# Delta rule: decay matrices kept in device memory, and four products tied into one run

## The chip, the cores and the metric

The kernel runs on one core of a Trainium2 chip. The metric is device time in microseconds, the median of three runs. A core has TensorE (PE in the profile, its weight loads PEld), VectorE (DVE), ScalarE (ACT), GpSimd (POOL) and SyncE (SP); each works through its own list of instructions in order. Here SyncE issues nearly all DMA transfers, and ScalarE a few.

## The reference

Two layers of a decoder trunk on 512 tokens of width 1024, all in float32. Each layer normalises x, makes one wide projection, and runs three branches side by side: a Mamba-2 scan, latent attention, and a gated delta rule. Their outputs are projected, gated, merged and projected again; a feed-forward part follows. The change lies in the delta rule, which in the reference has chunks of 64 tokens:

```
g = jnp.cumsum(chunks(g), axis=-1)
decay = jnp.exp(jnp.where(incl, g[..., :, None] - g[..., None, :], -jnp.inf))
a_mat = jnp.where(strict, jnp.einsum('bhcld,bhcmd->bhclm', kb, k) * decay, 0.0)
sol = lax.linalg.triangular_solve(a_mat + jnp.eye(L, dtype=jnp.float32), rhs, left_side=True, lower=True)
u, w = jnp.split(sol, [DV], axis=-1)
qk = jnp.where(incl, jnp.einsum('bhcld,bhcmd->bhclm', q, k) * decay, 0.0)
def step(state, inp):
    qc, kc, uc, wc, gc, ac = inp
    v_new = uc - jnp.einsum('bhld,bhdv->bhlv', wc, state)
    o = (jnp.einsum('bhld,bhdv->bhlv', qc * jnp.exp(gc)[..., None], state)
         + jnp.einsum('bhlm,bhmv->bhlv', ac, v_new))
    state = ...
```

So `decay` is used twice: in the matrix that is inverted (`a_mat`), and in the attention of queries to keys (`qk`).

## The kernel before, in words

The kernel uses chunks of 128 tokens, so T = 4 tiles of tokens, and treats the 8 heads of the delta rule in two units (u = 0, 1) of 4 heads. Weights come from device memory in pieces of 512 KB (`wraw`, two buffers, line 172), are split on ScalarE (line 159) and VectorE (line 160) into a high and a low part (`whi`, `wlo`, four buffers each), and are used in three matmuls for each product (lines 181 to 183, the dense matmuls). These take most of TensorE's time.

`seg_exp` (lines 452 to 460) makes the decay matrices of four heads for one tile of tokens. A mask is multiplied into the running sums on VectorE (L455, tile `sg`); one matmul of 128 x 512 in the reduced-precision float32 format gives all differences of running sums in a bank of the small PSUM ring (L457; the ring `sm` has three banks); two activations on ScalarE turn them into the decays (L459 and L460), which stand in a buffer `eE` of 128 x 512 float32, 256 KB. `eE` has two slots, used in turn by all who make such a tile: the delta rule here, the Mamba scan (`ssd_group`) and the inverses (`gdn_inverses`).

`gdn_matrix` (called for both units early in the layer) computes for each tile t the key products (L779, L783, L784), then calls `seg_exp` (L799), and multiplies decay, step size and key products on VectorE, once for each head (L802), into `nt`. Four small stores on SyncE's queue (L806) take parts of `nt` to device memory. `gdn_blocks` and `gdn_inverses` turn `nt` into the inverses.

`gdn_unit` runs much later, after most of the other two branches, once for each unit. It makes the queries, values and gates, and then loops over the tiles t in order, with a state `st` carried from tile to tile:

- the decay matrices are made again by `seg_exp` (L923);
- query-key products (L926), masked (L928) and multiplied with the decays (L930), in place, in the `eE` buffer;
- for t > 0, the state's part in the values (L935 on TensorE, L937 on VectorE, one instruction for each head h = 0 to 3);
- the products with the inverse `Y`, one for each head, plain float32 (two passes each), into one bank (L940);
- from that bank the new values: on VectorE (L942), and on ScalarE with the decay to the tile's end (L947); the next state (L950, L953 or L956);
- the output (L959, which reads the `eE` buffer, and L964, L965 or L969, L967), its squares on ScalarE (L973), a root on GpSimd (L261, called at L981) and the scaling with the gate on VectorE (L982, L985). After the loop the results are transposed (L990).

What sets the order: the Tile framework puts the instructions of each engine, and the DMAs of each queue, in one order when the kernel is built. [...] So dense matmuls of a neighbouring stage stand between the steps of a unit wherever the planner expected a wait. A buffer slot is given to its next writer when its last reader is done, and the waits are added by the framework. `tc.add_manual_dep(..., NoSync, ...)` fixes the order of two instructions and adds no wait.

Of the kernel before, what the change touches and what calls it, by code (L numbers as in the profile page):

```python
# [10 lines left out]
F32 = mybir.dt.float32  # L11
# [9 lines left out]
P = 128  # L21
S = 512
T = S // P
# [36 lines left out]
def hybrid_kernel(ctx, tc, a, out, depth=2, taps=None):  # L60
    nc = tc.nc
    pe, act, dve, pool, sync = nc.tensor, nc.scalar, nc.vector, nc.gpsimd, nc.sync
    uid = itertools.count()

    def mk(pl, shape, dt, tag, bufs=None):
        return pl.tile(shape, dt, tag=tag, name=f"{tag}_{next(uid)}", bufs=bufs)
# [22 lines left out]
    dr = ctx.enter_context(tc.tile_pool(name="dr", bufs=1, space=DRAM))  # L89
# [242 lines left out]
    for ly in range(depth):  # L332
# [119 lines left out]
        def seg_exp(pl, o, t, h0):  # L452

            w = mk(pl, [P, P], F32R, "sg", 2)
            dve.tensor_scalar(w, f32(cum[0][:, t]), sel[:, h0 // 4 : h0 // 4 + 1], None, ALU.mult)  # L455
            ps = sm_bank()
            pe.matmul(ps, w, cum[1][:, t].rearrange("p i l -> p (i l)"), start=True, stop=True)  # L457
            of = o.rearrange("p i l -> p (i l)")
            act.activation(of, ps, AF.Relu, scale=-1.0)  # L459
            act.activation(of, of, AF.Exp, scale=-1.0)  # L460
# [308 lines left out]
        def gdn_matrix(u):  # L769

            hd0 = 16 + 4 * u
            kT = key_tiles(4 + 2 * u)
            ssq = mk(sp, [P, 2, T], F32, "gss", 2)
            gks = []
            for t in range(T):
                tok = slice(t * P, (t + 1) * P)
                pg = sm_bank()
                for i in range(2):
                    pe.matmul(pg[:, i * P : (i + 1) * P], kT[i][:, tok], kT[i][:, tok], start=True, stop=True)  # L779
                gk = mk(br, [P, 2, P], F32, f"wk{t}")  # L780
                for i in range(2):

                    dve.scalar_tensor_tensor(gk[:, i], hv(pg)[:, i], 1.0, ident, ALU.mult, ALU.mult, accum_out=ssq[:, i, t : t + 1])  # L783
                dve.tensor_tensor(gk, hv(pg)[:, 0:2], bc_mid(nstrict, 2), ALU.mult)  # L784
                gks.append(gk)
            dve.tensor_scalar(ssq, ssq, 4.0 * EPS, None, ALU.add)
            ork = mk(sp, [P, 2, T], F32, "gork", 2)
            pool.tensor_tensor(ork.rearrange("p i t -> p (i t)"), ssq.rearrange("p i t -> p (i t)"), phalf[:, :8], ALU.pow)
            dve.tensor_scalar(ork, ork, 0.5, None, ALU.mult)
            rk2 = mk(sp, [P, 2, T], F32, "grk", 2)  # L790
            dve.reciprocal(rk2, ssq)
            cc = mk(sp, [P, T, 4], F32, "gcc", 2)
            for i in range(2):
                dve.tensor_tensor(cc[:, :, 2 * i : 2 * i + 2], beta[:, :, 4 * u + 2 * i : 4 * u + 2 * i + 2],
                                  bc_last(rk2[:, i, :], 2), ALU.mult)
            nt = mk(br, [P, T, 4, P], F32, "tok", 5)
            for t in range(T):
                e = mk(br, [P, 4, P], F32, "eE", 2)
                seg_exp(br, e, t, hd0)  # L799
                gk = gks[t]  # L800
                for h in range(4):
                    dve.scalar_tensor_tensor(nt[:, t, h], e[:, h], cc[:, t, h : h + 1], gk[:, h // 2], ALU.mult, ALU.mult)  # L802
            ntf = nt.rearrange("p t h n -> p (t h) n")
            for b in range(4):
                sl = slice(32 * b, 32 * b + 32)
                sync.dma_start(d_n[u][:, b].rearrange("h i j -> i h j"), ntf[sl, :, sl])  # L806
            cd = mk(sp, [P, T, 4], F32, "gcd", 2)
            dve.tensor_tensor(cd, cc, dec[:, 1, :, hd0 : hd0 + 4], ALU.mult)
            return kT, ork, cc, cd, nt
# [73 lines left out]
        def gdn_unit(u, kT, ork, cc, cd, Yt, yh, yl):  # L883
# [35 lines left out]
            for t in range(T):  # L919
                tok = slice(t * P, (t + 1) * P)  # L920
                Y = Yt[:, t]
                e = mk(br, [P, 4, P], F32, "eE", 2)
                seg_exp(br, e, t, hd0)  # L923
                pg = sm_bank()
                for i in range(2):
                    pe.matmul(pg[:, i * P : (i + 1) * P], kT[i][:, tok], qT[i][:, tok], start=True, stop=True)  # L926
                gk = mk(br, [P, 2, P], F32, "gk", 2)
                dve.tensor_tensor(gk, hv(pg)[:, 0:2], bc_mid(incl, 2), ALU.mult)  # L928
                pt_ = e
                dve.tensor_tensor(prs(pt_), prs(e), bc_j(gk), ALU.mult)  # L930
                r = v[:, t, :]
                if t > 0:
                    pk = sm_bank()
                    for i in range(2):
                        pe.matmul(pk[:, i * 256 : (i + 1) * 256], kT[i][:, tok], st[:, i * 256 : (i + 1) * 256], start=True, stop=True)  # L935
                    for h in range(4):
                        dve.scalar_tensor_tensor(hv(r)[:, h], hv(pk)[:, h], ndec[:, t, 4 * u + h : 4 * u + h + 1], hv(r)[:, h], ALU.mult, ALU.add)  # L937
                pw = sm_bank()
                for h in range(4):
                    pe.matmul(pw[:, h * P : (h + 1) * P], Y[:, h, :], r[:, h * P : (h + 1) * P], start=True, stop=True)  # L940
                vn = mk(br, [P, 512], F32, "wk1")
                dve.tensor_tensor(hv(vn), hv(pw), bc_last(cc[:, t, :], P), ALU.mult)  # L942
                sn = None
                if t < T - 1:
                    vd = mk(br, [P, 512], F32, "wk2")
                    for h in range(4):
                        act.activation(hv(vd)[:, h], hv(pw)[:, h], AF.Copy, scale=cd[:, t, h : h + 1])  # L947
                    pS = sm_bank()
                    for i in range(2):
                        pe.matmul(pS[:, i * 256 : (i + 1) * 256], ktok[i][:, t, :], vd[:, i * 256 : (i + 1) * 256], start=True, stop=True)  # L950
                    sn = mk(br, [P, 512], F32, "st", 2)
                    if t == 0:
                        act.copy(sn, pS)  # L953
                    else:
                        for h in range(4):
                            dve.scalar_tensor_tensor(hv(sn)[:, h], hv(st)[:, h], hdec(2, t, h), hv(pS)[:, h], ALU.mult, ALU.add)  # L956
                po = sm_bank()
                for h in range(4):
                    pe.matmul(po[:, h * P : (h + 1) * P], pt_[:, h, :], vn[:, h * P : (h + 1) * P], start=True, stop=True)  # L959
                o = mk(br, [P, 512], F32, "wk3")  # L960
                if t > 0:
                    pq = sm_bank()
                    for i in range(2):
                        pe.matmul(pq[:, i * 256 : (i + 1) * 256], qT[i][:, tok], st[:, i * 256 : (i + 1) * 256], start=True, stop=True)  # L964
                    act.copy(o, po)  # L965
                    for h in range(4):
                        dve.scalar_tensor_tensor(hv(o)[:, h], hv(pq)[:, h], hdec(0, t, h), hv(o)[:, h], ALU.mult, ALU.add)  # L967
                else:
                    act.copy(o, po)  # L969
                st = sn  # L970
                for h in range(4):
                    jk = mk(br, [P, P], F32, "gk", 2)
                    act.activation(jk, o[:, h * P : (h + 1) * P], AF.Square, accum_out=ss[:, t, h : h + 1])  # L973

                rqt = mk(sp, [P, 4], F32, "grt", 2)
                for j in range(2):
                    dve.tensor_scalar(rqt.rearrange("p (i j) -> p i j", j=2)[:, :, j], rq[:, :, t], 128.0 ** -0.5, None, ALU.mult)
                ms = mk(sp, [P, 4], F32, "gms", 2)
                dve.tensor_tensor(ms, ss[:, t, :], rqt, ALU.mult)
                dve.tensor_tensor(ms, ms, rqt, ALU.mult)  # L980
                rsq(ms, ms, 1.0 / 128, EPS)  # L981
                dve.scalar_tensor_tensor(ms, ms, 0.5, rqt, ALU.mult, ALU.mult)  # L982
                for h in range(4):
                    gzh = hv(gz[:, t, :])[:, h]
                    dve.scalar_tensor_tensor(gzh, gzh, ms[:, h : h + 1], hv(o)[:, h], ALU.mult, ALU.mult)  # L985
# [7 lines left out]

        cum[:] = cum_rows(br)
        d_n, d_x, d_y = (mk(dr, [2, 16, 4, 32, 32], F32, n, 2) for n in ("d_n", "d_x", "d_y"))
        mats = [gdn_matrix(u) for u in range(2)]
        nts = [m[4] for m in mats]
        blocks = gdn_blocks(nts)
# [299 lines left out]
```

## Time and profile before

| | |
|---|---|
| median of 3 runs | 2382.27 us (2379.41 to 2384.48) |
| profiled execution | 2376.62 us, its span 2374.8 us |
| granted TensorE clock | 0.993 |
| instructions | 32120 |
| DMA traffic | 214.90 MB, mean 90 GB/s |
| L457 on PE | 64 calls: 8 in each layer in `gdn_matrix`, 16 in `ssd_group`, 8 in `gdn_unit` |
| L940 on PE | 128 passes: 4 heads x 2 passes x 4 tiles x 2 units x 2 layers |
| `gdn_unit`'s tile loops | begin at 619, 701, 1797 and 1879 us |

Times in the views count from the start of the span. A row of the view in order of time has start, duration, engine, line, operation, output and inputs, shape and count of merged instructions; in square brackets stands the idle time of the engine before it and what ended that. PE's durations overlap, so the distance from one start to the next says what an instruction costs. A row of the waits has total us, number of times and the longest. A row of the DMA issues has the number, the size of one and the median time from issue to landing.

### The profile page before, as it was taken

Reading aid. Unit: us, or ns where it says so; the run is one execution under the profiler, and the core shown is the slowest. Engines: PE = TensorE matmul, PEld = TensorE weight load, DVE = VectorE, ACT = ScalarE, POOL = GpSimd, SP = SyncE. Lnnn points to the kernel's source line nnn. Section 1 sums busy time; section 2 is a strip of 40 time slices with the busy share of each in tenths; the row PEclk is TensorE's granted clock in tenths of the full one; section 3 lists DMA queues with packets and bytes.
Section 4 is the critical chain, followed back from the end, with each engine's and each line's share of the span. In section 5 each row is a group of like instructions: output and inputs, shape, how many; then the busy total and the mean of one; then the engine's idle time right before and its main releaser. Section 6 shows DMA issues by size and latency. Waiting matters only on the chain.

```text
span 2374.8 us, 32120 instructions
## 1 busy us (share of the span) xinstructions
PE 2331.7 (98%) x11984; PEld 1916.8 (81%) x11984; DVE 1598.0 (67%) x3180; ACT 1151.5 (48%) x2295; POOL 59.6 (3%) x76
## 2 busy tenths in 40 slices
PE   8999999999999999999999999999999999999998
PEld 6778778888887888888887777888887878888886
DVE  6778875635675468767857788656356655587668
ACT  6665534433454345554656555344235534455545
POOL 0000000000000000000000000000000000000000
PEclk9999999999999999999999999999999999999999
DMA  4322332233222443233132223322332224432231
GB/s 135 85 71 71 81 105 72 65 95 93 76 63 69 136 153 104 71 124 115 52 98 71 72 71 84 93 80 72 98 89 64 71 72 154 139 107 88 91 124 45
DMA packets 192445, 214.90 MB, mean 90 GB/s; under 512 B 30625, under 2 KB 151969, under 8 KB 192289
## 3 DMA queue, kind: packets, MB, share of 16 engines
q1 hardware_dynamic: 188768, 207.61, 28.8%
q10 hardware_dynamic: 3520, 5.25, 0.9%
q8 instruction: 94, 1.54, 0.3%
q14 instruction: 63, 0.51, 0.1%
HBM read 200.24 MB, written 7.34 MB: 87 GB/s over the span
## 4 chain that ended last, share of the span: by engine, by line
PE 92%; DVE 3%; ACT 2%; DMA 1%; POOL 1%; issue 1%; SPq 0%; ACTq 0%; POOLq 0%; DVEq 0%
PE acc L182 23%; PE acc L181 23%; PE acc L183 23%; PE sm L183 2%; PE sm L181 2%; PE sm L182 2%; PE sm L717 1%; PE sm L625 1%; PE sm L457 1%; PE yt L182 1%; PE yt L183 1%; PE yt L181 1%; PE sm L959 1%; DMA mix<-mix 1%; PE sm L940 1%
## 5 line engine op out<-in xcount | busy, mean ns | idle before, releaser
L159 ACT CAST whi<-wraw 128x512 fp32r<-128x512 f32 x552 | 342.0, 622 | 676.3 <-PE acc L182 470.8
L160 DVE TENSOR_TENSOR wlo<-wraw,whi 128x512 fp32r<-128x512 f32 x552 | 379.2, 689 | 427.6 <-ACT whi L159 421.8
L181 PE MATMUL acc<-xh,whi 128*128 128x512 f32 (+1 forms) x1184 | 462.1, 391 | 2.6 <-DVE vl L253 2.2
L182 PE MATMUL acc<-xl,whi 128*128 128x512 f32 (+1 forms) x1184 | 462.6, 391 | 0.0
L183 PE MATMUL acc<-xh,wlo 128*128 128x512 f32 (+1 forms) x1184 | 459.9, 389 | 0.0
L181 PEld LDWEIGHTS acc<-xh,whi 128*128 128x128 f32 x1184 | 223.4, 189 | 44.9 <-DVE vl L253 2.8
L182 PEld LDWEIGHTS acc<-xl,whi 128*128 128x128 f32 x1184 | 223.6, 189 | 43.8 <-issue 1.4
L183 PEld LDWEIGHTS acc<-xh,wlo 128*128 128x128 f32 x1184 | 223.6, 189 | 43.1 <-issue 1.4
L181 PE MATMUL acc<-yh,whi 128*128 128x512 f32 x384 | 152.1, 399 | 0.0
L182 PE MATMUL acc<-yl,whi 128*128 128x512 f32 x384 | 152.0, 396 | 0.0
L183 PE MATMUL acc<-yh,wlo 128*128 128x512 f32 x384 | 151.0, 393 | 0.0
L159 ACT CAST whi<-wr 128x512 fp32r<-128x512 f32 x160 | 99.6, 623 | 103.8 <-DVE wlo L160 37.5
L183 PE MATMUL acc<-whi,xl 128*128 128x512 f32 (+1 forms) x384 | 144.0, 376 | 0.0
L181 PE MATMUL acc<-whi,xh 128*128 128x512 f32 (+1 forms) x384 | 144.0, 377 | 0.0
L182 PE MATMUL acc<-wlo,xh 128*128 128x512 f32 (+1 forms) x384 | 143.4, 373 | 0.0
L160 DVE TENSOR_TENSOR wlo<-wr,whi 128x512 fp32r<-128x512 f32 x160 | 109.9, 688 | 27.7 <-ACT whi L159 27.6
L661 DVE SCALAR_TENSOR_TENSOR cva<-acc,pc,cva 128x511 f32<-128x511 f32 (+2 forms) x168 | 120.7, 743 | 11.1 <-ACT cva L657 7.6
L183 PE MATMUL acc<-whi,yl 128*128 128x512 f32 (+1 forms) x260 | 100.4, 386 | 0.0
L181 PE MATMUL acc<-whi,yh 128*128 128x512 f32 (+1 forms) x260 | 100.4, 386 | 0.0
L182 PE MATMUL acc<-wlo,yh 128*128 128x512 f32 (+1 forms) x260 | 100.3, 386 | 0.0
L181 PEld LDWEIGHTS acc<-yh,whi 128*128 128x128 f32 x384 | 71.6, 188 | 16.8 <-ACT yh L256 2.3
L182 PEld LDWEIGHTS acc<-yl,whi 128*128 128x128 f32 x384 | 72.3, 188 | 15.6 <-issue 1.4
(394 smaller groups left out, 4576.4 us busy)
## 6 DMA issues: line engine op xcount, KB each, us to landing
wraw<-in_w_in_dram SPq DMA_DIRECT2D x148, 512.0 KB, 3.7
wraw<-in_w_up_dram SPq DMA_DIRECT2D x64, 512.0 KB, 3.7
wr<-in_w_down_dram SPq DMA_DIRECT2D x32, 1024.0 KB, 5.1
wraw<-in_w_mla_out_dram SPq DMA_DIRECT2D x16, 512.0 KB, 3.5
wraw<-in_w_ssd_out_dram SPq DMA_DIRECT2D x16, 512.0 KB, 3.4
wraw<-in_w_gdn_out_dram SPq DMA_DIRECT2D x16, 512.0 KB, 3.4
wraw<-in_w_out_dram SPq DMA_DIRECT2D x16, 512.0 KB, 3.7
wraw<-in_mla_w_uq_dram SPq DMA_DIRECT2D x16, 384.0 KB, 3.5
```

The costliest lines, as they stand in the source:

```text
L159: act.copy(hi, raw)
L160: dve.tensor_tensor(lo, raw, f32(hi), ALU.subtract)
L181: pe.matmul(o, ah, bh, start=start, stop=False, skip_group_check=more)
L182: pe.matmul(o, ah, bl, start=False, stop=False, skip_group_check=more)
L183: pe.matmul(o, al, bh, start=False, stop=stop, skip_group_check=more)
L457: pe.matmul(ps, w, cum[1][:, t].rearrange("p i l -> p (i l)"), start=True, stop=True)
L625: pe.transpose(ps[:, n : n + P], pn[t][:, kb * P : (kb + 1) * P], ident)
L661: dve.scalar_tensor_tensor(acc[:, d:], ps[:, : S - d], taps_[3 - d], acc[:, d:], ALU.mult, ALU.add)
L717: pe.matmul(py[:, h * 64 : (h + 1) * 64], e2[h // 4][:, h % 4, :], xd[:, h * 64 : (h + 1) * 64], start=True, stop=True)
L940: pe.matmul(pw[:, h * P : (h + 1) * P], Y[:, h, :], r[:, h * P : (h + 1) * P], start=True, stop=True)
L959: pe.matmul(po[:, h * P : (h + 1) * P], pt_[:, h, :], vn[:, h * P : (h + 1) * P], start=True, stop=True)
```

## The change

Three edits. In `gdn_matrix` each tile's decay matrices are stored to a new array `d_e` in device memory, as soon as they are made, by a DMA on SyncE's queue. In `gdn_unit` `seg_exp` is no longer called; its result is loaded from `d_e` into an `eE` buffer, by a DMA on the same queue. And the four products with the inverse are issued for the heads 3, 2, 1, 0 in place of 0 to 3, with an order set by hand between one and the next. The arithmetic is the same.

```diff
 gdn_matrix, for t in range(T):
                 e = mk(br, [P, 4, P], F32, "eE", 2)
                 seg_exp(br, e, t, hd0)
+                sync.dma_start(d_e[u, t], e.rearrange("p i l -> p (i l)"))
 gdn_unit, for t in range(T):
                 e = mk(br, [P, 4, P], F32, "eE", 2)
-                seg_exp(br, e, t, hd0)
+                sync.dma_start(e.rearrange("p i l -> p (i l)"), d_e[u, t])
...
                 pw = sm_bank()
-                for h in range(4):
-                    pe.matmul(pw[:, h * P : (h + 1) * P], Y[:, h, :], r[:, h * P : (h + 1) * P], start=True, stop=True)
+                prev = None
+                for h in (3, 2, 1, 0):
+                    m = pe.matmul(pw[:, h * P : (h + 1) * P], Y[:, h, :], r[:, h * P : (h + 1) * P], start=True, stop=True)
+                    if prev is not None:
+                        tc.add_manual_dep(m.ins, prev, mybir.DependencyInfo(mybir.DependencyClass.NoSync, mybir.DependencyReason.DATA),
+                                          reason="in_order")
+                    prev = m.ins.name
 the layer's body, once for each layer:
         d_n, d_x, d_y = (mk(dr, [2, 16, 4, 32, 32], F32, n, 2) for n in ("d_n", "d_x", "d_y"))
+        d_e = mk(dr, [2, T, P, 512], F32, "d_e", 2)
```

`d_e` has an array for each layer, with 2 units x 4 tiles of 256 KB. So 16 stores and 16 loads of 256 KB come in over the whole kernel, and 16 of the 64 calls of `seg_exp` go.

## Prediction

> **What bounds the kernel now.** I read the page first: its span, its busy times, and the chain that ended last.
>
> ```profile
> span 2374.8 us, 32120 instructions
> ...
> PE 2331.7 (98%) x11984; PEld 1916.8 (81%) x11984; DVE 1598.0 (67%) x3180; ACT 1151.5 (48%) x2295; POOL 59.6 (3%) x76
> ...
> PE 92%; DVE 3%; ACT 2%; DMA 1%; POOL 1%; issue 1%; SPq 0%; ACTq 0%; POOLq 0%; DVEq 0%
> ```
>
> TensorE (PE) is busy for 98% of the span and makes 92% of the chain. So an edit is worth what it takes out of PE's stream or out of PE's gaps, and work taken from ScalarE (48%) counts only where PE waits for it. The profiled execution took 2376.62 us: 2374.8 of span and 1.8 around it. The median of the three runs is 2382.27, 5.65 more; I make the sum on 2376.62 and carry the difference over. A measurement of this kernel can tell about 0.2% (4.8 us) from no change.
>
> The unit that the change edits is entered at about 619 us in the first layer; PE in order of time there:
>
> ```profile
> 618.82 0.39 PE L183 MATMUL acc<-whi,xl 128*128 128x512 f32 x1
> 619.04 0.39 PE L457 MATMUL sm<-cm,sg 128*128 128x512 f32 x1
> 619.27 0.60 PE L926 MATMUL sm<-ft,ft 128*128 128x128 f32 x4
> 619.71 1.06 PE L940 MATMUL sm<-tok,tok 128*128 128x128 f32 x8
> 620.53 0.48 PE L181 MATMUL acc<-xh,whi 128*128 128x512 f32 x1
> ```
>
> The second column, 0.39, is a pipelined duration; what a matmul costs is the distance to the next start. A dense one (L183) costs 0.22, the decay's exponent (L457) 0.23, and the four heads' products with the inverse (L940, eight passes, two a head) 0.82 in one run. At t = 0 they are in one run already. Then the whole list of waits:
>
> ```profile
> ACT whi L159 <- PE acc L182: 489.4, 312, 5.7
> ...
> PEld sm L940 <- DVE tok L937: 7.4, 18, 0.7
> ...
> PE yt L990 <- DVE tok L985: 3.0, 4, 0.9
> ```
>
> The columns are total us, times, longest. ScalarE's weight casts wait 489 us for PE to give buffers back, so the weights are ahead of PE. The weight load of L940 waits 18 times for the vector update of L937 in front of it; that is the only stall here that the tie touches.
>
> **The change part by part.**
>
> *The recomputation that goes.* In `gdn_unit`, 2 layers x 2 units x 4 tiles = 16 calls of `seg_exp` go, and with each one L457 on PE, one mask multiplication (L455) on VectorE, and the two activations L459 and L460 on ScalarE. PE: 16 x 0.23 = 3.7 us. The lower end is the dense distance, 16 x 0.22 = 3.5; the upper is the full 0.39, 16 x 0.39 = 6.2, if nothing overlapped. I take 3.7, since the row at 619.04 has dense work before and f32 work after it and shows the distance itself. ScalarE gets back 16 x (0.59 + 0.63) = 19.5 us (the two kinds in the rows of ScalarE below), which I count at nothing: its time is hidden by PE, as the casts' 489 us of waiting show. A bank of the small PSUM ring is also taken 16 times less.
>
> *The tie.* PE and the vector engine at t = 1 of the first unit, and PE at t = 2:
>
> ```profile
> 627.91 0.39 PE L182 MATMUL acc<-xl,whi 128*128 128x512 f32 x1
> 628.13 0.38 PE L940 MATMUL sm<-tok,tok 128*128 128x128 f32 x2
> 628.27 0.48 PE L183 MATMUL acc<-xh,wlo 128*128 128x512 f32 x1
> 628.59 0.39 PE L181 MATMUL acc<-xh,whi 128*128 128x512 f32 x1
> ...
> 629.43 0.47 PE L181 MATMUL acc<-xh,whi 128*128 128x512 f32 x1
> 630.24 0.49 PE L940 MATMUL sm<-tok,tok 128*128 128x128 f32 x2 [0.34 <-DVE tok L937]
> ...
> 640.05 0.40 PE L183 MATMUL acc<-xh,wlo 128*128 128x512 f32 x1
> 640.48 0.49 PE L940 MATMUL sm<-tok,tok 128*128 128x128 f32 x2
> ```
>
> ```profile
> 629.76 0.16 DVE L982 SCALAR_TENSOR_TENSOR gms<-gms,grt 128x4 f32<-128x4 f32 x1 [0.87 <-POOL gms L261]
> 629.84 0.34 DVE L937 SCALAR_TENSOR_TENSOR tok<-sm,ndec,tok 128x128 f32<-128x128 f32 x1
> ```
>
> At t = 1 to 3 each head's product is issued on its own between dense matmuls. Does that cost anything by itself? From L182 at 627.91 to L181 at 628.59 is 0.68; two dense distances (0.22 to 0.23) leave 0.23 for the head. Four in a run cost 0.82, and the first dense matmul after f32 passes has a distance of 0.32 (628.27 to 628.59) in place of 0.23, which makes 0.91, or 0.23 a head. Run or not is the same price: the tie saves no PE work.
>
> What it can save is waiting. At 629.43 PE issues a dense matmul and then stands in front of the fourth head: 0.81 to the next start, where 0.32 would do, so 0.5 is lost. The vector rows say why: the fourth L937 stands behind L982, which waited 0.87 for GpSimd. At t = 2, 0.43 against 0.23: 0.2 lost. With about 0.2 at t = 3 as well, a unit loses 0.9, and four units 3.6. All of it can go, if the planner puts the run where the fourth update is really done; none of it goes if the run is put where the fourth head now stands, since head 3 comes first and the three others wait behind it. Below nothing it goes only by the rival on the run's length. What becomes shorter for certain is the vector stream in front of the fourth update, by one mask multiplication (some 0.28 us: the rows above show 128x128 operations of 0.34). That covers the 0.2 at t = 2 and 3 and half of the 0.5 at t = 1: 0.68 a unit, 2.7 for four. The planner may spend the freed time on something else, so I take half: 1.4. What is late next is the vector update after the product (L942), which now waits for all four heads; dense matmuls of the next weights fill PE meanwhile.
>
> *The store.* 16 stores of 256 KB join SyncE's queue in `gdn_matrix`. None exists before; the nearest rows are the kernel's other stores, the output with the same size and the residual with twice that:
>
> ```profile
> hd<-h SPq DMA_DIRECT2D x4, 512.0 KB, 3.0
> h<-hd SPq DMA_DIRECT2D x4, 512.0 KB, 5.8
> out_dram<-h SPq DMA_DIRECT2D x8, 256.0 KB, 2.2
> ```
>
> So 2.2 to 3.0 us from issue to landing. The decay buffer `eE` has two slots, and a slot is now free only when its store has landed. ScalarE in both units of the first layer:
>
> ```profile
> 236.75 0.63 ACT L460 ACTIVATE eE<-eE 128x512 f32<-128x512 f32 x1
> ...
> 242.33 0.59 ACT L459 ACTIVATE eE<-sm 128x512 f32<-128x512 f32 x1
> ...
> 246.18 0.60 ACT L459 ACTIVATE eE<-sm 128x512 f32<-128x512 f32 x1 [2.60 <-DVE tok L802]
> ...
> 255.06 0.63 ACT L460 ACTIVATE eE<-eE 128x512 f32<-128x512 f32 x1
> ...
> 257.94 0.59 ACT L459 ACTIVATE eE<-sm 128x512 f32<-128x512 f32 x1
> ```
>
> Unit 0: the first matrix is done at 237.38, its store has landed by 239.6 to 240.4, and the slot is written next at 242.33: hidden behind the vector products that hold the slot anyway. Unit 1: done at 255.69, landed by 257.9 to 258.7, written at 257.94: late by 0 to 0.8 us. Behind a waiting L459 on ScalarE stand weight casts. They bear it: at 246.18 ScalarE already waited 2.60 for a slot, and over the span the casts wait 489 us for PE and not PE for them. I cost the store at nothing; without that cover it would be 0.8 x 2 layers = 1.6.
>
> *The load.* 16 loads of 256 KB on SyncE, each waiting until the L959 of two tiles before has read the slot, with weight loads queued behind it. For t = 2 the slot is free before 628.13, where PE is at the inverse products of t = 1, since L959 of t = 0 stands ahead of them on PE. The slowest row, 5.8 us for twice the size, gives 633.9; the matrix is wanted by L959 of t = 2, which comes after the products at 640.48. It is hidden, and L930 finds its matrix early. A weight load queued behind such a load waits at most until L959, which is work of the same stage; the casts' waiting on PE covers that. Cost: nothing; at worst, as in the second rival.
>
> Sum: 3.7 + 1.4 = 5.1 us off. 2376.62 - 5.1 = 2371.5 for a profiled execution, and 2382.27 - 5.1 = 2377.2 for the median.
>
> **The rivals.**
>
> *The tie gives nothing.* The manual order says only that head 3 comes before 2, 1 and 0; a dense matmul may still stand between them, and PE may wait for the fourth update as now. Then only L457 is gone: -3.7, or 2378.6, within 0.2%. For it: the 0.87 wait for GpSimd stays in the vector stream. Against it: 0.28 us of vector work in front is gone. If the run's later end also costs something the gain shrinks towards nothing: its three earlier heads (3 x 0.23 = 0.7 us) now run after the last update, and where no dense work is at hand that is 0.7 lost; in five of the twelve steps it would eat the 3.7.
>
> *The store holds the PSUM bank: slower.* L457 of the next matrix writes one of three small PSUM banks and keeps it until L459 has read it; L459 waits for the slot, and so for the store. SyncE's queue before:
>
> ```profile
> 242.50 7.30 SPq L172 DMA_DIRECT2D wraw<-in_w_in_dram  x2
> ```
>
> If the planner queues a store behind the weight load that starts at 242.50 only when its buffer is free, the store goes out at 242.9 and lands at 245.1 to 245.9: L459 comes 2.8 to 3.6 us later than its 242.33. From the point where PE's next small product needs that bank, PE stands still, whatever weights are ready. At 3 us a unit, four units cost 12: net +6.9, or 2389.2. For it: in unit 0 the slots are a wait already (2.60). Against it: the matrix is done at 237.38, five us ahead of that load, so a queue in the order of real time has the store first. [...]
>
> *More stalls go.* If the whole 3.6 of the L940 stalls goes, and with a shorter vector and ScalarE stream also the 3.0 that PE waits at L990 for the end of the units: 3.7 + 3.6 + 3.0 = 10.3, or 2372.0. For it: these are the waits of just these loops. Against it: the GpSimd wait is untouched, and the planner re-orders what follows.
>
> **How the numbers follow.** The forecast has 0.41 (its own spread 2374.5 to 2380; 0.27 of it beyond 0.2% and 0.14 within), the tie without effect 0.26 (within), more stalls gone 0.18 (faster), the held bank 0.15 (slower). Faster 0.27 + 0.18 = 0.45; same 0.14 + 0.26 = 0.40; slower 0.15. The range goes from 2371 (just under the best sum) to 2387, which takes in a held bank of up to 2.5 us a unit and leaves out about 0.15 at the ends.
>
> **What would show it.** Right: L457, L459 and L460 48 times each, not 64; L940 as one row x8 at all t; the wait of L940 for L937 shorter; L930 waiting for no DMA; PE's instructions down by 16. Wrong: ScalarE at L459 waiting for a store in `gdn_matrix` with a gap on PE beside it (held bank); a gap of 0.5 or more in front of the L940 run (tie without effect); a PE wait for a weight cast (a queue of SyncE that the loads block); or PE's order changed in stages that the change doesn't touch.

## The result, and the profile after

| | median us | runs | span of the profiled run | its granted clock |
|---|---|---|---|---|
| before | 2381.38 | 2379.41 to 2384.48 | 2374.8 | 0.993 |
| after | 2367.78 | 2363.07 to 2374.19 | 2372.4 | 0.994 |

The ratio is 0.9946, 95% interval 0.9930 to 0.9961: the kernel is faster by 13.6 us, 0.39 to 0.70%. The forecast was 5.1 us and the range ended at 2371. One thing must be known before the two profiles are laid side by side. The profiled run of after took 2374.19 us, the slowest of its five; the other four ran at a mean clock of 0.996 to 0.998 and took 2363.07 to 2367.98. So this pair of traces shows 2.4 us of the 13.6, and what is missing must be looked for in the clock. One run of a later experiment, the store alone, took 3305.46 us at a granted clock of 0.653, and its ratio leaves that run out.

Line numbers of after are one higher than before behind L799, two at the products with the inverse (L940 is L942), six or seven behind them.

The page of after, and the instructions of L457:

```profile
span 2372.4 us, 32119 instructions
...
PE 2325.4 (98%) x11968; PEld 1916.5 (81%) x11968; DVE 1594.8 (67%) x3164; ACT 1133.6 (48%) x2263; POOL 61.4 (3%) x76
...
PE 91%; DVE 3%; ACT 2%; DMA 1%; POOL 1%; issue 1%; SPq 0%; ACTq 0%; POOLq 0%; DVEq 0%
```

```profile
L457 PE MATMUL sm<-cm,sg x48: 389/392/799, 239.7 to 1614.9; 128*128 128x512 f32 x48
```

PE has 16 instructions fewer, ScalarE 32 and VectorE 16, and L457 stands 48 times. The edit did what it says. The new transfers and what SyncE waits for (total us, times, longest):

```profile
d_e<-eE SPq DMA_DIRECT2D x16, 256.0 KB, 2.1
eE<-d_e SPq DMA_DIRECT2D x16, 256.0 KB, 2.7
```

```profile
SPq L924 <- PE sm L965: 49.4, 12, 5.4
...
SPq L800 <- ACT eE L460: 38.6, 16, 4.6
```

2.1 and 2.7 us to landing; 2.2 to 3.0 were forecast. SyncE does stand in front of the stores (L800) and the loads (L924) with weight loads queued behind it, 38.6 us at the stores and, with three smaller rows for L924, 72.6 at the loads. Little of it arrives at ScalarE: its casts wait for the input projection's weights 3.0 us in three places, 1.5 us in three before. Its longest wait for a decay product grows, not in the matrix stage but in the Mamba scan behind it, which calls `seg_exp` too (4.15 us at 287.09, and the same in layer 2):

```profile
ACT eE L459 <- PE sm L457: 13.2, 10, 4.2
...
ACT whi L159 <- DMA wraw<-in_w_in_dram: 3.0, 3, 1.8
```

(6.7 us in 16 waits at L459, none over 0.5, before. In the matrix stage the longest wait at L459 is 2.60 us in both kernels.) The tie ties in all 16 tiles, and the stall that it was to remove is still there. All four heads in one row, with the wait ahead of them:

```profile
634.19 1.13 PE L942 MATMUL sm<-tok,tok 128*128 128x128 f32 x8 [0.57 <-DVE tok L938]
```

In groups by line, products with the inverse and their weight loads (busy, mean ns, then idle time just before and what ended it):

```profile
L942 PE MATMUL sm<-tok,tok 128*128 128x128 f32 x128 | 17.7, 281 | 3.2 <-DVE tok L938 3.1
L942 PEld LDWEIGHTS sm<-tok,tok 128*128 128x128 f32 x128 | 15.5, 191 | 7.4 <-ACT whi L159 3.8 <-issue 1.9 <-PE acc L183 1.7
```

PE itself waits 3.1 us for VectorE's L938 there, 1.4 for the same line before; its weight loads wait 7.4 us in all, 10.8 before, and where they waited for L937 they now wait behind weight casts (L159). By start distances (what goes beyond 0.31 us behind a dense product and 0.11 behind another head), with excesses under 0.05 left out, PE loses 4.7 us in front of these products before and 4.6 after. Many small waits have become fewer and larger ones.

**The units by themselves.** The stage that the change edits begins with the sums of squares (L891, L892 after) and ends with the first transposes of the next normalization (L292). Layer 1, before and then after, the first start in each row:

```profile
L891 PE MATMUL sm<-ct,ft x16: 164/250/250, 577.9 to 579.8; 128*128 128x1 f32 x16
...
L292 PE MATMUL sm<-ct,xr x16: 270/272/276, 849.5 to 853.0; 128*128 128x128 f32 x16
```

```profile
L892 PE MATMUL sm<-ct,ft x16: 164/250/250, 581.6 to 583.5; 128*128 128x1 f32 x16
...
L292 PE MATMUL sm<-ct,xr x16: 270/272/282, 850.6 to 854.1; 128*128 128x128 f32 x16
```

849.5 - 577.9 = 271.6 becomes 850.6 - 581.6 = 269.0. In layer 2 the same distance goes from 271.7 to 269.0. So both layers give 2.6 + 2.7 = 5.3 us. The forecast for exactly this was 5.1. The units hold what was predicted, and 8.3 us of the 13.6 come from somewhere else.

**Where the clock goes.** Windows of 10 us over the inverses (`gdn_inverses`) of layer 1; the column behind the engines' busy times is PEclk, the granted clock. Before:

```profile
350.00:360.00 10.00, 10.00 (x156) 7.93 (x154) 2.83 (x5) 3.30 (x5) 0.00 (x0) 1.00 0.01 2
360.00:370.00 10.00, 9.11 (x124) 8.18 (x117) 7.93 (x13) 6.33 (x11) 0.00 (x0) 0.69 0.08 13
370.00:380.00 10.00, 10.00 (x78) 7.97 (x77) 1.39 (x2) 3.68 (x7) 0.00 (x0) 0.80 0.26 95
```

0.31 and 0.20 of two windows are missing, 5.1 us of full clock. They lie in one stretch: a window over 363.8 to 374.0 alone shows PEclk 0.50, and 2 x 5.1 = 10.2 us is its length. Layer 2 has the same at 1541. PE's instructions that lead to it, in order of time:

```profile
360.09 1.14 PE L876 MATMUL sm<-bA,tok 64*64 64x64 f32 x16
361.90 0.97 PE L880 MATMUL sm<-tok,eE 64*64 64x64 f32 x13 [0.67 <-ACT eE L877]
...
362.98 1.39 PE L865 MATMUL sm<-tok,eE 32*32 32x32 f32 x32
364.29 1.75 PE L876 MATMUL sm<-bA,tok 64*64 64x64 f32 x14
366.26 0.79 PE L181 MATMUL acc<-xh,whi 128*128 128x512 f32 x1 [0.22 <-ACT whi L159]
...
371.67 0.63 PE L182 MATMUL acc<-xl,whi 128*128 128x512 f32 x1
372.09 0.63 PE L183 MATMUL acc<-xh,wlo 128*128 128x512 f32 x1
```

From the dense product at 358.64 to the one at 366.26 PE runs only blocks of 32x32 and 64x64 for 7.4 us, with two waits of 0.67 and 0.22 us among them. At 363.8 the clock halves, and dense products that stand 0.23 apart elsewhere stand 0.42 apart (371.67 to 372.09). The profiled run of after has the same length of half clock, which is why it shows so little:

```profile
360.00:370.00 10.00, 9.66 (x152) 8.30 (x151) 5.96 (x9) 4.78 (x8) 0.00 (x0) 0.79 0.01 4
370.00:380.00 10.00, 10.00 (x60) 8.00 (x59) 4.72 (x8) 3.51 (x7) 0.00 (x0) 0.70 0.35 105
```

But PE's order has changed there, in a function that the diff doesn't touch. In both layers before has, by the program's order, 8 dense products, then the last level's blocks, and the next dense one only behind five runs of blocks. After has 12 dense products there and two more behind the second run:

```profile
364.25 0.50 PE L182 MATMUL acc<-xl,whi 128*128 128x512 f32 x1
364.58 0.40 PE L183 MATMUL acc<-xh,wlo 128*128 128x512 f32 x1
365.32 1.58 PE L881 MATMUL sm<-tok,eE 64*64 64x64 f32 x16 [0.34 <-ACT eE L878]
```

**Two theories** stood then. The gate theory, on TensorE's granted clock: some two thirds of the gain is time at half clock; the changed order of the inverses makes the stretch at half clock a thing of some runs and not of all. The work theory, the rival: the gain is the removed L457 with its ScalarE passes, and the clock is a by-product.

### The profile page after: what moved, and what is told of

Same layout as the page of the kernel before. It is cut to its first block, busy times and chain, and to the rows that moved or that the text cites. A ratio compares the mean times of both kernels' runs of the same rounds, so it can differ in the third digit from the quotient of the medians.

```text
span 2372.4 us, 32119 instructions
## 1 busy us (share of the span) xinstructions
PE 2325.4 (98%) x11968; PEld 1916.5 (81%) x11968; DVE 1594.8 (67%) x3164; ACT 1133.6 (48%) x2263; POOL 61.4 (3%) x76
## 4 chain that ended last, share of the span: by engine, by line
PE 91%; DVE 3%; ACT 2%; DMA 1%; POOL 1%; issue 1%; SPq 0%; ACTq 0%; POOLq 0%; DVEq 0%
PE acc L182 23%; PE acc L181 23%; PE acc L183 23%; PE sm L181 2%; PE sm L182 2%; PE sm L183 2%; PE sm L717 1%; DMA mix<-mix 1%; PE sm L625 1%; PE sm L942 1%; PE yt L182 1%; PE yt L181 1%; PE yt L183 1%; PE sm L965 1%; PE sm L292 1%
## 5 line engine op out<-in xcount | busy, mean ns | idle before, releaser
L159 ACT CAST whi<-wraw 128x512 fp32r<-128x512 f32 x552 | 341.9, 622 | 663.9 <-PE acc L182 464.0
L159 ACT CAST whi<-wr 128x512 fp32r<-128x512 f32 x160 | 99.6, 622 | 103.7 <-DVE wlo L160 37.5
L183 PEld LDWEIGHTS acc<-yh,wlo 128*128 128x128 f32 x384 | 72.4, 188 | 15.2 <-issue 1.0
```

The costliest lines, as they stand in the source:

```text
L159: act.copy(hi, raw)
L183: pe.matmul(o, al, bh, start=False, stop=stop, skip_group_check=more)
```

## The experiments

Ratios are against runs of the kernel before on the same chip; four kernels share a chip. The median of before on the four chips was 2378.48, 2380.53, 2380.12 and 2378.09.

**1. The two kernels again, and the change in halves.** The first two are the kernels unchanged. The third has the store and the load, with the products with the inverse as before; the fourth has the tie alone.

```
store_load_only: the two dma_start lines and d_e, without the loop over (3, 2, 1, 0)
tie_only:        the loop over (3, 2, 1, 0) with its add_manual_dep, seg_exp in the unit as before
```

> The kernel before, unchanged, to see the granted clock of each execution. The gate theory (two thirds of the 13.6 us between the medians are half-clock stretches of TensorE in the inverses, which the kernel before meets in nearly every execution and the changed one in some): clocks of 0.993 to 0.994 in nearly all runs at 2377 to 2384 us; a run that shows 0.997 is 7 to 9 us faster. The work theory (the changed kernel simply issues 13 us less work and waits): clocks spread as in the changed kernel, 0.994 to 0.998, and times of 2377 to 2384 at all of them.

Measured: 2379.29 (2376.87 to 2394.90), ratio 1.0009 [0.9995, 1.0023]; clock 0.993 or 0.994 in most runs, 0.991 in two at 2383.58 and 2385.52, 0.988 in the one at 2394.90.

> The changed kernel, unchanged. The gate theory: times go with the granted clock, about 2374 us at 0.994 and 2362 at 0.998, some 2.8 us for each 0.001; at the clock of the kernel before it is 5 to 7 us faster. The work theory: 2363 to 2374 without a relation to the clock, 13 us below the kernel before at equal clock.

Measured: 2365.67 (2364.77 to 2367.92), ratio 0.9946 [0.9932, 0.9959], clock 0.996 to 0.998. The gain and the clock repeat. That times go with the clock from run to run, as the gate theory expected, these six do not show: 2364.77 and 2366.03 at 0.996, 2364.85 and 2365.86 at 0.998.

> The decay matrices through device memory, the four products as before (heads 0 to 3, no order set). The prediction's sum: 3.7 us less than before at equal clock, the stalls ahead of the inverse products as before (0.5 at t = 1, 0.2 at t = 2 and 3). The gate theory for the median: if moving the inverses by some us is what misses the half-clock stretches, this kernel too is 8 to 12 us faster in the median. The work theory: the part of 13 that is not the tie's, 4 to 9 us.

Measured: 2364.81 (2362.59 to 2369.11), ratio 0.9942 [0.9928, 0.9956], clock 0.996 to 0.999. Its profiled run has no half clock except in the last 8 us of the kernel; its mean clock is 0.999.

> The four products tied as in the change, the decay matrices computed twice as before. The prediction's sum: 1.4 us faster (0 to 3.6). The gate theory: nothing ahead of the inverses in layer 1 changes, so the half-clock stretch there comes as in the kernel before; in layer 2 the inverses come earlier by the tie's gain of layer 1. Median within 3 us of before. The work theory: 4 to 9 us faster at equal clock.

Measured: 2383.33 (2377.97 to 2393.38), ratio 1.0011 [0.9996, 1.0025], clock 0.988 to 0.994.

The whole gain, with its clock, hangs on store and load; PE's order in the inverses is that of after in store_load_only, that of before in tie_only. The medians can't tell the tie from nothing. The units can, since their length repeats to about 0.2 us from run to run. Tie alone, then store and load alone:

```profile
L891 PE MATMUL sm<-ct,ft x16: 164/250/250, 582.7 to 584.5; 128*128 128x1 f32 x16
...
L292 PE MATMUL sm<-ct,xr x16: 270/273/276, 854.9 to 858.4; 128*128 128x128 f32 x16
```

```profile
L892 PE MATMUL sm<-ct,ft x16: 164/250/250, 575.9 to 577.8; 128*128 128x1 f32 x16
...
L292 PE MATMUL sm<-ct,xr x16: 270/272/275, 845.6 to 849.1; 128*128 128x128 f32 x16
```

Both layers together: before 543.3, tie alone 544.7, store and load 539.5 (269.76 + 269.78), after 538.0. So store and load are worth 3.8 us there, and the tie costs 1.4 by itself and gains 1.5 where the load is there. By the same count as above PE loses 2.8 us in front of the products with the inverse in tie_only and 5.9 in store_load_only. So the tie does shorten the stall, 4.7 to 2.8 alone and 5.9 to 4.6 beside the load; before and after look alike only because it is longer with store and load. Alone the tie pays elsewhere: PE waits for the last vector updates of the units (L985 of before) 6.5 us in eight waits, 3.0 in four before.

**2. The store alone, and order alone.** The store of the matrix stage with the units computing as before:

```
+                sync.dma_start(d_e[u, t], e.rearrange("p i l -> p (i l)"))
+        d_e = mk(dr, [2, T, P, 512], F32, "d_e", 2)
```

> The matrix stage stores the decay matrices, but the units compute them again as before, untied: all of the old work plus sixteen stores. The planner's PE order in the inverses is then the one of the kernel after (12 dense products where before has 8, and two more between the first blocks of the last level), longest stretch without a dense product about 3.8 us instead of 7.3 us. Gate theory (most of the gain is time at half clock that no longer follows those small blocks): mean clock 0.996 or more and about 2368.5 us, the 2364.8 of store and load without the tie plus 3.7 for the second L457. Work theory (the gain is the removed product and its two ScalarE passes): the time of before, 2377 to 2382, at the clock of before, 0.993 to 0.994.

Measured: 2369.70 (2366.91 to 2373.62, but for the run named with the result), ratio 0.9955 [0.9939, 0.9972], clock 0.996 to 0.999, units 543.2. Its profiled run, at 0.996, still has 6.8 us at half clock in the inverses of each layer. All the old work is there, and 10.8 us are gained. The order in the inverses is that of after, so it is the store that moves the planner; the load has no part in it.

The kernel before with one priority changed:

```
-        ssd_group(0, *ys)
+        with tc.high_priority(-20):
+            ssd_group(0, *ys)
```

> The kernel before with all its work, the first Mamba group alone given 20 steps less priority in the planner. PE's order changes only in and just ahead of the inverses, where the longest stretch without a dense product is now two runs of blocks, then three (about 2.2 and 3.4 us) instead of 7.3 us. Gate theory: the half-clock stretch of 10 us that each layer of before shows there is gone or rarer, mean clock 0.996 or more, 2366 to 2373 us. Work theory: nothing is removed, so 2376 to 2382 us as before, whatever the clock does.

Measured: 2370.90 (2367.23 to 2371.99), ratio 0.9955 [0.9939, 0.9972], clock 0.998 or 0.999 in every run, units 543.4. Nothing is removed, no transfer is added, and 9.6 us are gone. PE's order differs from before only in the inverses and some 300 matmuls ahead of them, which belong to the same Mamba group. The same windows, and the same blocks:

```profile
360.00:370.00 10.00, 10.00 (x143) 8.48 (x136) 6.19 (x10) 6.45 (x12) 0.00 (x0) 1.00 0.09 18
370.00:380.00 10.00, 10.00 (x86) 8.32 (x85) 5.19 (x8) 5.48 (x10) 0.00 (x0) 1.00 0.40 119
```

```profile
360.17 1.14 PE L876 MATMUL sm<-bA,tok 64*64 64x64 f32 x16
361.24 0.50 PE L181 MATMUL acc<-xh,whi 128*128 128x512 f32 x1
...
362.04 0.39 PE L181 MATMUL acc<-xh,whi 128*128 128x512 f32 x1
362.36 0.91 PE L880 MATMUL sm<-tok,eE 64*64 64x64 f32 x12
363.20 1.19 PE L865 MATMUL sm<-tok,eE 32*32 32x32 f32 x32
...
365.41 0.50 PE L182 MATMUL acc<-xl,whi 128*128 128x512 f32 x1
```

Four dense products from 361.24 on break the blocks, and the clock stays at 1.00. The work theory falls here. Another rival is that the new order saves waits and not clock. From PE's 1.19 us wait at L457 in layer 1 to the same wait in layer 2 before takes 1177.85 us and this kernel 1171.73; PE's busy time goes from 1165.77 to 1160.12. So of the 6.1 us only 0.5 is waiting: the same matmuls take PE less time.

**3. How many dense products it takes.** Store and load with the two loops of the last level exchanged, so that the longest stretch without a dense product gets shorter by the order:

```
-            for u in range(2):
-                for i0 in (0, 8):
+            for i0 in (0, 8):
+                for u in range(2):
```

> Store and load without the tie, and the two loops over group and half in the inverses' last level exchanged: the same work, the longest stretch without a dense product now about 2.3 us instead of 3.8 us. Gate theory: no half-clock time inside the inverses in any execution, clock 0.998 or more in all, 2361 to 2364 us, one to three us under store and load with the old loops, and a narrower spread. Work theory: the same 2364.8 us.

Measured: 2370.85 (2369.39 to 2373.74), ratio 0.9961 [0.9947, 0.9975], clock 0.995 to 0.997 in all eight runs. A miss: slower than the old loops, and the clock halves more often.

```profile
360.00:370.00 10.00, 9.66 (x149) 7.81 (x148) 6.38 (x10) 5.71 (x10) 0.00 (x0) 0.75 0.01 4
370.00:380.00 10.00, 10.00 (x78) 7.99 (x76) 3.79 (x6) 3.07 (x6) 0.00 (x0) 0.74 0.37 105
```

```profile
363.36 0.50 PE L182 MATMUL acc<-xl,whi 128*128 128x512 f32 x1
363.70 0.40 PE L183 MATMUL acc<-xh,wlo 128*128 128x512 f32 x1
364.44 1.50 PE L881 MATMUL sm<-tok,eE 64*64 64x64 f32 x16 [0.34 <-ACT eE L878]
365.87 1.91 PE L866 MATMUL sm<-tok,eE 32*32 32x32 f32 x32
367.70 0.80 PE L181 MATMUL acc<-xh,whi 128*128 128x512 f32 x1
```

Two dense products at 363.36 and 363.70 with 2.3 us of blocks in front of them, and the clock halves at 365.0 all the same. So here it isn't the longest stretch without a dense product that counts. The shortest time at half clock in the trace of before is 3.4 us (at 1292). In the 3.4 us ahead of a stretch in the inverses stood no dense product in before and two in after, in both layers each, two here, and three in experiment 4; where four stood in such a place (before_spread), neither layer of the profiled run has a stretch (PEclk 1.00 in all windows from 330 to 390 and from 1510 to 1560). Two are not always too few: the profiled run of store_load_only has the order of after in the inverses, two dense products included, and no stretch in either layer (mean clock 0.999).

The kernel after with one run of dense products pushed back in layer 1 alone:

```
-        gdn_inverses(nts, blocks)
+        with tc.high_priority(5000):
+            gdn_inverses(nts, blocks)
```

> The kernel after with all its work, the inverses given 5000 steps more priority: in layer 1 alone 21 dense products move behind the following blocks, so that five runs of blocks (about 6 us) follow each other without a dense product; layer 2 keeps the order of after. Gate theory: a half-clock stretch of about 10 us in layer 1's inverses in every execution, mean clock 0.995 to 0.996, 2368 to 2372 us. Work theory: nothing is added, so 2365 to 2367 us as the kernel after.

Measured: 2370.62 (2368.07 to 2374.54), ratio 0.9963 [0.9946, 0.9979], clock 0.994 to 0.997. This lies in the gate theory's range, and the profiled run has 10.2 us at half clock in layer 1 (PEclk 0.91 and 0.58 from 360 to 380) and none in layer 2 (1.00 from 1530 to 1550). Of the gain over before 9.9 us are left, where after had 13.6 and 12.8. It is weak evidence by itself: after was not run on this chip, the intervals overlap, and after too can have 10.2 us there.

**4. A version with more dense work between the blocks.** Store and load, the loops exchanged, and 60 steps less priority for the first Mamba group; store and load once more as its yardstick.

> Store and load without the tie, the two loops of the inverses' last level exchanged and the first Mamba group given 60 steps less priority: the same work, and every stretch of 3.4 us in the inverses holds by the order at least three dense products, where it held two or fewer in the versions whose clock halved. Gate theory in its second form (it is the dense work of 3.4 us that counts, not the longest stretch without any): no half-clock time inside the inverses in any execution, clock 0.998 or more in all, 2361 to 2365 us, zero to four us under store and load with the old order. Work theory: the time of store and load, whatever the order.

Measured: 2367.65 (2366.29 to 2369.63), ratio 0.9946 [0.9934, 0.9959], clock 0.997 to 0.999.

> Store and load without the tie, once more, on the chip of the other three: by its order the clock halves in some executions and not in others, mean clock 0.996 to 0.999, 2363 to 2370 us. It is the yardstick for the version with the spread order. Both theories say the same here.

Measured: 2367.44 (2363.32 to 2370.23), ratio 0.9942 [0.9929, 0.9955], clock 0.996 to 0.999.

The clock came nearly as expected (one stretch of 3.4 us stands at the very start of layer 1's inverses, PEclk 0.92 and 0.91 from 330 to 350), the time didn't: narrower, not lower. At 0.998 or 0.999 the new order takes 2366.3 to 2367.8, the old one 2363.3 to 2367.4. So the order that keeps the clock up may cost up to 3 us by itself (the two ranges overlap), and no version here beats store and load as the change has them.

**5. Without the inverses.** The call of `gdn_inverses` is left out in each of these six kernels, which leaves out the last two levels of the block inverses, so that what is left of a difference has nothing to do with their order.

> The kernel before without the call of the inverses in both layers: leaves out the last two levels of the block inverses, some 38 us of small blocks on PE. Gate theory: no half-clock time between 300 and 450 us of either layer's stage, clock 0.998 or more, 2328 to 2340 us. It is the yardstick for the next.

Measured: 2348.39, ratio 0.9864 [0.9850, 0.9877], clock 0.994 to 0.996. Neither was expected: the clock still halves at 360 us (PEclk 0.54 from 360 to 365, 0.77 from 365 to 370), without those blocks, and the kernel is slower than thought: the blocks had filled a true wait of PE, which now stands open.

```profile
359.36 0.63 PE L696 MATMUL sm<-ct,ft 128*128 128x128 f32 x4 [3.93 <-DVE ft L265]
```

> The kernel after without the call of the inverses, which leaves out the same levels. With no stretch of small blocks in either kernel the clock can't make the difference, so what is left is the edit's own worth. Gate theory: 3 to 6 us under the kernel before without the inverses (3.7 for the second L457, 0 to 1.4 for the tie, something for ScalarE in the matrix stage), both at clock 0.998 or more. Work theory: the whole 12 to 14 us of the two full kernels.

Measured: 2341.57, ratio 0.9833 [0.9820, 0.9847], clock 0.995 or 0.996: 6.8 us less than its yardstick at nearly the same clock, where 3 to 6 were expected of the gate theory and 12 to 14 of the work theory. The clock is not quite out of it: the profiled run has 6.8 us at half clock in each layer, the yardstick's 6.8 and 10.2.

> The kernel before without the inverses, once more, as the yardstick of the other three on one chip: 2346 to 2349 us at clock 0.994 to 0.996 (both layers keep one half-clock stretch, where PE waits 3.9 us for the convolution on VectorE).

Measured: 2350.87, ratio 0.9880 [0.9864, 0.9896], clock 0.994.

> Without the inverses, the matrix stage stores, the units compute again as before. By the prediction's sum the store costs nothing: the yardstick's time within 1 us. Rival (the store also changes PE's order in the matrix and Mamba stages, and that is worth something): 2 to 4 us under the yardstick.

Measured: 2346.19, ratio 0.9857 [0.9839, 0.9876], clock 0.996: 4.7 us less, where the prediction's sum has nothing. But from PE's wait of 1.2 us at L457 to the wait of 3.9 us the trace has 114.2 us in the yardstick and 113.7 here, 0.5 a layer, and the units are equal (543.8 and 543.5). The rest lies around the open wait, where both layers have 6.8 us at half clock in place of 10.2. So by these traces the store's own worth is about 1 us.

> Without the inverses, store and load, no tie. By the prediction's sum 3.7 us under the version with the store alone (sixteen L457 at 0.23). If the removed ScalarE passes or the DVE behind them had been on the path too, 5 us or more under it.

Measured: 2343.17, ratio 0.9849 [0.9833, 0.9865], clock 0.995 or 0.996: 3.0 us less than with the store alone, 3.7 expected.

> Without the inverses, the tie alone. By the prediction's sum 1.4 us under the yardstick; by the first rival nothing, within 0.7 us of it.

Measured: 2349.29, ratio 0.9874 [0.9855, 0.9893], clock 0.994 or 0.995: 1.6 us under its yardstick, with ranges that overlap. Its units take 544.7 us, 0.9 more than the yardstick's, so this difference isn't the tie's. Its profiled run has 6.8 us at half clock in layer 2, where the yardstick has 10.2.

## Why the prediction was wrong

The direction was right and the size was not; the time fell below the range.

- *The removed recomputation: right in size, in part by luck.* 16 x 0.23 = 3.7 was the forecast; store and load shorten the units by 543.3 - 539.5 = 3.8. But the stall in front of the products with the inverse grew by 1.2 us with it (4.7 to 5.9), so something else gave about as much back. What that was is not known.
- *The tie: the amount and the place right, the reason not.* 1.4 was forecast and 1.5 found beside store and load, and 1.3 of it is the stall (5.9 us, then 4.6). But the forecast counted on the mask multiplication that goes to shorten the stall "for certain", and with it gone the stall grew. Alone the tie costs 1.4, because PE then waits longer at the units' end.
- *Load and store at no cost: right, and wrong by its silence.* The held bank (rival 2) did not come: PE waits 1.5 us in two waits at L457 in layer 1's matrix stage, as before. Yet the store alone moved the time by 10.8 us.
- *The sum: the failed step.* It was made over the edited stages alone, at the clock of the profiled run, and what a changed order elsewhere might do was named as a sign of error and priced at nothing. The profile of before showed what was at stake: 20.5 us at half clock in the inverses, where the windows have PEclk 0.69 and 0.80. No row of PEclk stands in the prediction.
- *The third rival, more stalls go, 2372.0:* nearest in time, and not what happened.

How the 13.6 us come together. Between two like points, PE's 1.19 us wait at L457 in layer 1 and in layer 2; before, after, and store and load:

```profile
238.81 0.91 PE L457 MATMUL sm<-cm,sg 128*128 128x512 f32 x2 [1.19 <-DVE sg L455]
...
1416.66 0.50 PE L457 MATMUL sm<-cm,sg 128*128 128x512 f32 x1 [1.19 <-DVE sg L455]
```

```profile
242.78 0.92 PE L457 MATMUL sm<-cm,sg 128*128 128x512 f32 x2 [1.19 <-DVE sg L455]
...
1417.43 0.91 PE L457 MATMUL sm<-cm,sg 128*128 128x512 f32 x2 [1.19 <-DVE sg L455]
```

```profile
241.47 0.91 PE L457 MATMUL sm<-cm,sg 128*128 128x512 f32 x2 [1.19 <-DVE sg L455]
...
1409.48 0.91 PE L457 MATMUL sm<-cm,sg 128*128 128x512 f32 x2 [1.19 <-DVE sg L455]
```

1177.85, 1174.65 and 1168.01 us. The first two runs have the same 13.6 us at half clock (10.2 in the inverses, 3.4 at 1292 and 1291), so 3.2 us of a layer is the edit: 2.6 in the units, about 0.5 in the matrix stage. The third has none, and is 6.6 us shorter than the second, although its units are 0.8 longer for want of the tie: 7.4 for 13.6, about half a microsecond for each one at half clock. Two layers of edit make 6.4, near the 6.8 us that after_noinv is under its yardstick. The mean clock went from 0.993 to 0.997 (medians of before_again and after_again), which is 0.004 x 2377 = 9.5 us of full clock, if PE sets the end all the time. 6.4 and at most 9.5 stand against 13.6. The 2.3 us between lie within the intervals, and not all of the clock's part need reach the end.

Two things stay open. Why the store makes the planner start the inverses six dense products earlier was not followed. And whether the clock halves in a given run of after is not settled by its order: the same program has 10.2 us in each layer in the profiled run, at a mean clock of 0.994, and other runs at 0.996 to 0.998.

## What to carry to other kernels

Where TensorE makes nine tenths of the chain, read the granted clock by windows before pricing an edit: a stage in which it falls is a term of its own, and any edit that lets a planner reorder that stage can move it by more than the edit is worth. In a stage of small blocks, look how much dense work stands between them: with four 128x512 products in 3.4 us the clock stayed at 1.00 here (before_spread), with two it stayed up in store_load_only (mean 0.999) and halved in after (0.50 for 10.2 us in each layer). And compare a stage with itself between two like points of two traces: the units took 543.2 and 543.3 us in two profiled runs of before and 543.2 and 543.4 in two kernels that leave them alone, while twelve runs of before ranged over 18 us.

## What the runs showed of the hardware that was not expected

The clock halved where PE was busy all the time, in store_load_spread at 338.5 us, behind blocks of 32x32 with three dense products among them (the window's PE busy time is 10.00 of 10 us, its PEclk 0.92):

```profile
330.00:340.00 10.00, 10.00 (x103) 7.92 (x102) 7.79 (x14) 3.52 (x6) 0.00 (x0) 0.92 0.72 124
```

In before PE did wait 0.67 us in the 3.4 us ahead of 363.8 and was busy 2.74 of them. That wait does not explain it by itself: from 237.48 to 240.89 of the same trace PE was busy only 2.22, with dense products, and the clock stayed at 1.00.

Two dense products among the blocks did not settle it: the profiled run of after, with two, has 10.2 us at half clock in each layer, that of store_load_only, in the same order, none (mean clock 0.999). In the traces of before and after the stretches away from the kernel's end last 3.4 us (at 1292 and 1291) or 10.2 us (in the inverses of both layers), and in before_noinv one lasts 6.8 us: 3.4 once, twice and three times. What sets this length, and why the same order shows a stretch in one run and none in another, was not shown. Nor is it idle time of PE alone that halves the clock here: the row above has none, and before and before_spread run the same blocks, the one at PEclk 0.69 and 0.80 from 360 to 380, the other at 1.00. Behind PE's wait of 3.93 us without the inverses the clock halved too, for 6.8 us in layer 1 of before_noinv (PEclk 0.54 and 0.77).
